# Where operand tiles land, the order of a block's seven products, an in-place tanh, and the order of matmuls and mixer steps in a hybrid decoder layer

## The chip, the core and the metric

The kernel runs on one core of one Trainium2 chip. The metric is the device time of one execution in microseconds (us). Three executions of the kernel before took 2190.18 (median), 2188.14 and 2193.57 us. One further execution was recorded by the hardware profiler; it took 2188.96 us, of which the profile's span covers 2186.9 us.

## What is computed

One decoder layer over 2048 tokens of width 1024, in float32, followed by a final norm:

```python
h = modulate(rmsnorm(x, norm1_w), shift1, scale1)
proj = h @ w_in                                  # q, k, v, z, xbc, dt
attn = sliding_window_attention(rope(q), rope(k), v, sinks)    # window 128
xbc  = silu(causal_depthwise_conv(xbc, conv_w, conv_b))
y    = ssd_chunked_scan(xs, dt, A, Bm, Cm, d_skip)             # chunks of 128
y    = group_rmsnorm(y * silu(z)) * ssm_norm_w
x    = x + gate1 * (concat([attn, y]) @ w_out)
h = modulate(rmsnorm(x, norm2_w), shift2, scale2)
g, u = split(h @ w_gate_up)                      # 1024 -> 2 x 2816
x    = x + gate2 * ((silu(g) * u) @ w_down)
out  = rmsnorm(x, final_norm_w)
```

Shifts, scales and gates come from a small projection of `c`. The change touches the projection `z` (the "gates" below), and the first of the two feed-forward products, `h @ w_gate_up`.

## The kernel before

**Tiles and numbers.** The tokens are worked on in four blocks of 512 (`T`). A float32 product is made of three matmuls on pairs of reduced-precision tiles: an operand is split into a high part (the copy, ScalarE) and a low part (the rest, mostly VectorE), and `mm3` or `product` adds high*high, high*low and low*high in one PSUM bank. So every operand costs one ScalarE instruction and one VectorE or GpSimd instruction per 128x512 tile: `halves` for weights (L897 the high part, L898 the low part), `kept` (L931, L932) and `shifted` (L926, L927) for the feed-forward operands.

**Projections and the mixer beside them.** For each block, the projections (queries, keys and values, convolution, gates) run as generators that stop (`yield`) after each piece. Between two pieces, `tick(ratio)` advances the mixer's generators by `ratio` steps on average: attention and the state-space scan of an earlier block. Of attention, a step transposes the keys (L623, into the PSUM bank `am`) and the queries (L628, bank `at`), ScalarE and VectorE split both (L624 and L625 to the tile `k_ring`, L631 and L632 to a tile `m`), and the scores follow (L663, banks `am` and `at`). VectorE masks the scores (L672), ScalarE takes exponentials and scales them (L685, L691), the probabilities are transposed (L697 on TensorE, copied out of PSUM by ScalarE at L699) and multiplied by the values (L706, copied out at L708). L791 and L806 are the scan's matmuls, L735 and L736 its running sums, L208 a product of the adaLN projection that VectorE makes beside all this, L850/L851 and L278/L279 splits of other operands.

**The gates.** `gated(b, h)` makes z for a block in `two_parts`: two passes over half of the depth, each of two parts of two pieces. A piece has 24 matmuls, and the first pass has four pieces. Each finished 128x256 tile goes through ScalarE (tanh, L538) and VectorE (L539) and is stored to memory (L540). The tanh went to a tile of the ring "s", which has three buffers of 128x512 and serves the convolution, the rotary embedding and the feed-forward's sums too; L539's result went to a staged tile "so" of a ring of six.

**The feed-forward's quads.** `quad(s, f, ...)` makes one 512-wide column block f (22 of them) for a pair s of token blocks (s=0: blocks 0 and 1, s=1: blocks 2 and 3) in a seven-product scheme of the Strassen kind. It loads four weight tiles (L903), forms sums of them (L1059, L1060, L1064, L1066, tiles of the ring "s" ), splits them into seven pairs w11, w12, ws1..ws4, w22 (L897, L898), and multiplies each with one of seven operands (b11, b21, t1, t2, t3, b22, t4): 7 x 12 matmuls of 128x512 on L1049, L1050 and L1051. ScalarE copies out the first product (L1073), a tanh of the second (L1077), and the third product (L1081). With `fresh`, which was set for f=0 of both pairs, the last four products are written k by k rather than product by product. For s=0 the operands b11, b21 and t1 are ready early, and the other four (t2, t3, b22, t4) are computed ahead and wait in memory: for k=0..2 as `raw_d`, for k=3 in tiles of the ring "t" (eight buffers, `tmp()`). `operands_kept` loads them after quad 0 has been begun: three tiles of t2 into three tiles of the ring "t" (L1015), then their conversions, then three tiles of t3, and so on. Weight loads of quad 1 are issued after the last of these loads.

**What sets the order.** On TensorE the order up to the end of block 3's gates is the order of the code (`tc.manual_schedule`, L1544). From the quads on, and on the other engines nearly everywhere, a scheduler with a timeline model orders the instructions of each engine; a tile that comes out of a ring has to wait until the last reader of the buffer's earlier content is done. Around the gates of block 2 the code was: `take(g, 4)`, that is, all four pieces of the first pass, and then four times `tick(MIX2)`. MIX2 is 1.1: so many mixer steps each tick makes on average. PSUM has four banks "d" for the dense products and one each of `am`, `at`, `sm`, `st` for the mixer.

Of the kernel before, what the change touches and what calls it, by code (L numbers as in the profile page):

```python
# [45 lines left out]
def hymba_layer(ctx, tc, xT, xtok, pos, wada, wadk, vecs, rows, wq, wkv, wz, wx, wo, wgu, wd, outT):  # L46
# [11 lines left out]
    def big(tag, bufs, dt=F32, pool=sb):  # L58
        return pool.tile([P, T], dt, name=tag, tag=tag, bufs=bufs)
# [14 lines left out]
    def tmp():  # L74
        return big("t", TMP, pool=fw)
# [315 lines left out]
    def staged():  # L391
        return small([P, 256], "so", 6, pool=ip)
# [141 lines left out]

    def gated(b, h):
        def gate(part, t, ps):
            z, th = staged(), big("s", 3, pool=fw)[:, 0:256]
            nc.scalar.activation(th, ps, AF.Tanh, scale=0.5)  # L538
            nc.vector.scalar_tensor_tensor(z, th, 1.0, ps, ALU.add, ALU.mult)  # L539
            nc.sync.dma_start(z_d[b * NT + t][:, part * 256:part * 256 + 256], z)  # L540
        yield from two_parts(b, h, "z", wz, gate)

# [351 lines left out]
    def halves(x, eng):  # L894
        two = wt.tile([P, 2, 528], F32R, name="w", tag="w", bufs=SPLIT)
        hi, lo = two[:, 0, 0:T], two[:, 1, 0:T]
        nc.scalar.activation(hi, x, AF.Copy)  # L897
        eng.tensor_tensor(lo, x, hi.bitcast(F32), ALU.subtract)  # L898
        return hi, lo
# [29 lines left out]
    def kept(into, x, eng=nc.gpsimd):  # L929
        hi, lo = into  # L930
        nc.scalar.activation(hi, x, AF.Copy)  # L931
        eng.tensor_tensor(lo, x, hi.bitcast(F32), ALU.subtract)  # L932
# [75 lines left out]
                yield  # L1008

    def operands_kept(ops):  # L1010
        for n, src in zip(("t2", "t3", "b22", "t4"), (2, 1, 0, 3)):
            got = []
            for k in range(3):
                x = tmp()
                scaled.last = nc.sync.dma_start(x, raw_d[k][src])  # L1015
                got.append(x)
            for k, x in enumerate((*got, sums_ahead.last[n])):
                if n == "b22":
                    shifted(ops[n][k], x, shift_of(k, 1))
                else:  # L1020
                    kept(ops[n][k], x, nc.gpsimd if n == "t4" else nc.vector)

    def operands_last(s, ops, bc):

# [19 lines left out]
    def product(out, a, b, first, ks=range(4)):  # L1044
        for k in ks:
            ks = slice(k * P, (k + 1) * P)
            ahi, alo = a[0][:, ks], a[1][:, ks]
            bhi, blo = b[k]
            nc.tensor.matmul(out, ahi, bhi, start=first and k == 0, stop=False, skip_group_check=True)  # L1049
            nc.tensor.matmul(out, ahi, blo, start=False, stop=False, skip_group_check=True)  # L1050
            mm3.last = nc.tensor.matmul(out, alo, bhi, start=False, stop=k == 3, skip_group_check=True)  # L1051

    def quad(s, f, ops, banks, fresh, behind):
        with tc.issue_after(scaled.last.ins) if behind else nullcontext():
            a11, a21, a22, a12 = (load_w(wgu[f, u, half]) for u, half in ((0, 0), (1, 0), (1, 1), (0, 1)))
        w11 = halves(a11, nc.vector)
        w12 = halves(a12, nc.vector)
        s1, s2, s3, s4 = (big("s", 3, pool=fw) for _ in range(4))
        nc.vector.tensor_tensor(s1, a21, a22, ALU.add)  # L1059
        nc.vector.tensor_tensor(s2, s1, a11, ALU.subtract)  # L1060
        ws1 = halves(s1, nc.vector)
        ws2 = halves(s2, nc.vector)
        other = nc.gpsimd if s else nc.vector
        other.tensor_tensor(s3, a11, a21, ALU.subtract)  # L1064
        ws3 = halves(s3, nc.vector)
        other.tensor_tensor(s4, a12, s2, ALU.subtract)  # L1066
        ws4 = halves(s4, nc.vector)
        w22 = halves(a22, nc.vector)

        pa, pb, pc, pd = banks  # L1070
        u2, u3, c22 = tmp(), tmp(), tmp()
        product(pa, w11, ops["b11"], True)
        nc.scalar.activation(u2, pa, AF.Copy)  # L1073
        yield
        product(pa, w12, ops["b21"], False)
        g1, g2 = tmp(), tmp()
        nc.scalar.activation(g1, pa, AF.Tanh, scale=0.5)  # L1077
        nc.vector.scalar_tensor_tensor(g1, g1, 1.0, pa, ALU.add, ALU.mult)
        yield
        product(pc, ws1, ops["t1"], True)  # L1080
        nc.scalar.activation(c22, pc, AF.Copy)  # L1081
        yield
        turns = ((pb, ws2, "t2", True), (pd, ws3, "t3", True), (pc, ws4, "b22", False), (pa, w22, "t4", True))
        if fresh:
            for k in range(4):
                for out, w, name, new in turns:
                    product(out, w, ops[name], new, (k,))
                if k < 3:
                    yield

        def turn(i):
            if not fresh:
                out, w, name, new = turns[i]
                product(out, w, ops[name], new)

        def keep(name, x):
            nc.sync.dma_start(act_d[s][name][f // 2], x)
        turn(0)
        nc.vector.tensor_tensor(u2, u2, pb, ALU.add)
        yield  # L1100
        turn(1)
        nc.vector.tensor_tensor(u3, u2, pd, ALU.add)
        nc.gpsimd.tensor_tensor(c22, c22, u3, ALU.add)
        yield
        turn(2)
        nc.vector.tensor_tensor(u2, u2, pc, ALU.add)
        nc.scalar.activation(g2, u2, AF.Tanh, scale=0.5)
        nc.vector.scalar_tensor_tensor(g2, g2, 1.0, u2, ALU.add, ALU.mult)
        nc.gpsimd.tensor_tensor(g2, g2, c22, ALU.mult)
        if f % 2:  # L1110
            b11, b12 = held[s]
            keep("b22", g2)
            nc.vector.tensor_tensor(b12, g2, b12, ALU.subtract)
            keep("t3", b12)
            nc.vector.tensor_tensor(b11, b11, b12, ALU.add)
            keep("t2", b11)
        yield
        turn(3)
        nc.vector.tensor_tensor(u3, u3, pa, ALU.add)
        nc.vector.tensor_tensor(g1, g1, u3, ALU.mult)  # L1120
        if f % 2:
            keep("b21", g1)
            nc.vector.tensor_tensor(u3, g1, b11, ALU.subtract)
            keep("t4", u3)
        else:
            keep("b11", g1)
            nc.vector.tensor_tensor(u3, g2, g1, ALU.subtract)
            keep("t1", u3)
            held[s] = g1, g2
        yield  # L1130
# [413 lines left out]
    with tc.manual_schedule(engines={mybir.EngineType.PE}):  # L1544
# [31 lines left out]
        finish(mix0)  # L1576
        mix = []
        g = gated(2, h)
        take(g, 4)
        for _ in range(4):  # L1580
            tick(MIX2)
        split = mixed(0, mix, range(KT), lambda c: operand())
        for _ in beside(g, MIX1):
# [53 lines left out]
    def quads(s, ops, banks, behind, before_last=None):  # L1637
        for f in range(NF):
            if before_last and f == NF - 1:
                before_last()  # L1640
            yield from quad(s, f, ops, banks(f), f == 0, f == behind)

    bp = early.enter_context(tc.tile_pool(name="b0l", bufs=1, reuse_waits="tile"))
    operand_tiles(ops, bp, ("b22", "t3", "t2", "t4"))
# [172 lines left out]
```

## Time and profile before

| | |
|---|---|
| three runs | 2190.18 (median), 2188.14, 2193.57 us |
| profiled execution | 2188.96 us, span 2186.9 us |
| granted TensorE clock, mean | 0.993 |
| TensorE busy (matmul) | 2140.5 us, 98% of the span |
| VectorE busy | 1669.6 us, 76% |
| ScalarE busy | 1017.8 us, 47% |
| GpSimd busy | 547.5 us, 25% |
| DMA | 466.76 MB, mean 213 GB/s |

TensorE is PE in the views, VectorE DVE, ScalarE ACT, GpSimd POOL; SPq is the queue from which SyncE issues transfers. A row of the timeline is: start, duration, engine, line, operation, the tiles written and read, the shape, how many; and in brackets the idle time of the engine before it with the instruction that ended it. Matmuls are pipelined: a row's duration is the time of one through the array, and the distance between two starts is what one costs.

### The profile page before, as it was taken

The numbers are of one execution on the slowest core, as the hardware profiler recorded it, in microseconds if no ns is written. First come the engines' busy times: TensorE is split into PE (matmuls) and PEld (weight loads), VectorE is DVE, ScalarE is ACT, GpSimd is POOL, SyncE is SP. The second block draws the span as 40 slices with busy tenths as digits, with TensorE's granted clock in tenths as the row PEclk, the third lists the DMA queues.
The fourth block names the chain that finished last, engine by engine and source line by source line (L and its number), as shares of the span: only waits on it lengthen the run. The fifth ranks groups of instructions, "written<-read, shape, count | busy, mean of one in ns | idle before, by whom it ended". The sixth has DMA issues, their size and how long they took to land.

```text
span 2186.9 us, 33266 instructions
## 1 busy us (share of the span) xinstructions
PE 2140.5 (98%) x10984; PEld 1763.5 (81%) x10984; DVE 1669.6 (76%) x3195; ACT 1017.8 (47%) x2137; POOL 547.5 (25%) x658
## 2 busy tenths in 40 slices
PE   8989999899999999999999999999999999999998
PEld 6888897788777777778888888788888888788887
DVE  7978857875777876789888679778888775786575
ACT  3776635653556545334344445433333334554441
POOL 0213443222111211243331222333333230210011
PEclk8999999999999999999999999999999999999999
DMA  7798988797998322333324778645555536678553
GB/s 280 240 341 309 345 267 296 243 334 239 356 361 294 116 99 89 125 102 122 125 92 159 243 259 286 226 138 190 171 171 181 167 115 233 231 259 281 184 163 103
DMA packets 287708, 466.76 MB, mean 213 GB/s; under 512 B 27440, under 2 KB 97072, under 8 KB 287536
## 3 DMA queue, kind: packets, MB, share of 16 engines
q1 hardware_dynamic: 286960, 464.13, 63.5%
q8 instruction: 86, 1.41, 0.3%
q14 instruction: 86, 0.70, 0.1%
q10 hardware_dynamic: 576, 0.52, 0.1%
HBM read 329.73 MB, written 134.81 MB: 212 GB/s over the span
## 4 chain that ended last, share of the span: by engine, by line
PE 79%; DVE 9%; DMA 6%; ACT 3%; issue 3%; POOL 1%; SPq 0%; DVEq 0%; ACTq 0%; POOLq 0%
PE d L1181 15%; PE d L1049 9%; PE d L1050 9%; PE d L1051 9%; PE d L286 5%; PE d L287 5%; PE d L288 5%; PE d L1322 1%; PE am L1051 1%; PE am L1049 1%; PE am L1050 1%; PE am L706 1%; DMA a<-act_t 1%; PE sm L1051 1%; PE sm L1050 1%
## 5 line engine op out<-in xcount | busy, mean ns | idle before, releaser
L1181 PE MATMUL d<-a,w 128*128 128x512 f32 x1716 | 402.3, 395 | 3.6 <-DVE w L1177 2.1
L1181 PEld LDWEIGHTS d<-a,w 128*128 128x128 f32 x1716 | 321.8, 188 | 81.3 <-DVE w L1177 2.9
L1049 PE MATMUL d<-b,w 128*128 128x512 f32 x924 | 366.1, 399 | 5.0 <-ACT t L1081 3.0
L1050 PE MATMUL d<-b,w 128*128 128x512 f32 x924 | 367.4, 398 | 0.2 <-DVE b L932 0.2
L1051 PE MATMUL d<-b,w 128*128 128x512 f32 x924 | 366.2, 398 | 0.2 <-DVE w L898 0.2
L1049 PEld LDWEIGHTS d<-b,w 128*128 128x128 f32 x924 | 174.1, 188 | 45.2 <-ACT t L1081 3.5
L1050 PEld LDWEIGHTS d<-b,w 128*128 128x128 f32 x924 | 174.3, 189 | 40.8 <-DVE b L932 0.8
L1051 PEld LDWEIGHTS d<-b,w 128*128 128x128 f32 x924 | 173.9, 188 | 39.4 <-DVE w L898 0.5
L897 ACT ACTIVATE w<-s 128x512 fp32r<-128x512 f32 x176 | 110.9, 632 | 203.2 <-PE d L1051 146.0
L286 PE MATMUL d<-w,hl 128*128 128x256 f32 (+1 forms) x592 | 172.1, 291 | 2.7 <-DVE s L511 2.7
L287 PE MATMUL d<-w,hl 128*128 128x256 f32 (+1 forms) x592 | 167.2, 282 | 0.0
L288 PE MATMUL d<-w,hl 128*128 128x256 f32 (+1 forms) x592 | 167.0, 282 | 0.0
L898 DVE TENSOR_TENSOR w<-s,w 128x512 fp32r<-128x512 f32 x176 | 156.9, 893 | 7.1 <-ACT w L897 5.9
L1163 DVE TENSOR_TENSOR a<-a 128x512 fp32r<-128x512 f32 x154 | 112.0, 739 | 49.2 <-ACT a L1162 48.8
L897 ACT ACTIVATE w<-raw 128x512 fp32r<-128x512 f32 x132 | 83.1, 631 | 132.5 <-PE d L1051 54.1
L1177 DVE TENSOR_TENSOR w<-raw,w 128x512 fp32r<-128x512 f32 x156 | 109.8, 713 | 39.0 <-ACT w L1176 37.0
L1162 ACT ACTIVATE a<-a 128x512 fp32r<-128x512 f32 x154 | 95.6, 628 | 88.8 <-DMA a<-act_t 50.9
L296 POOL TENSOR_TENSOR acc<-acc,t 128x512 f32<-128x512 f32 x35 | 52.5, 1499 | 319.6 <-ACT t L295 308.9
L286 PE MATMUL d<-hl,w 128*128 128x512 f32 x320 | 131.6, 411 | 0.3 <-DVE stp L565 0.3
L1176 ACT ACTIVATE w<-raw 128x512 fp32r<-128x512 f32 x156 | 90.6, 587 | 84.3 <-PE d L1181 51.5
L288 PE MATMUL d<-hl,w 128*128 128x512 f32 x320 | 126.1, 394 | 0.0
L287 PE MATMUL d<-hl,w 128*128 128x512 f32 x320 | 125.8, 393 | 0.0
(421 smaller groups left out, 4782.0 us busy)
## 6 DMA issues: line engine op xcount, KB each, us to landing
raw<-in_wgu_dram SPq DMA_DIRECT2D x176, 256.0 KB, 2.9
act_t<-t SPq DMA_DIRECT2D x88, 256.0 KB, 3.1
a<-act_t SPq DMA_DIRECT2D x88, 256.0 KB, 4.3
act_b<-t SPq DMA_DIRECT2D x66, 256.0 KB, 2.0
a<-act_b SPq DMA_DIRECT2D x66, 256.0 KB, 4.2
aw<-in_wada_dram SPq DMA_DIRECT2D x64, 256.0 KB, 5.1
w<-w_x SPq DMA_DIRECT2D x32, 512.0 KB, 5.7
raw<-wd_s SPq DMA_DIRECT2D x64, 256.0 KB, 3.0
```

The costliest lines, as they stand in the source:

```text
L286: nc.tensor.matmul(out, ahi, bhi, start=first, stop=False)
L287: nc.tensor.matmul(out, ahi, blo, start=False, stop=False)
L288: mm3.last = nc.tensor.matmul(out, alo, bhi, start=False, stop=last)
L897: nc.scalar.activation(hi, x, AF.Copy)
L898: eng.tensor_tensor(lo, x, hi.bitcast(F32), ALU.subtract)
L1049: nc.tensor.matmul(out, ahi, bhi, start=first and k == 0, stop=False, skip_group_check=True)
L1050: nc.tensor.matmul(out, ahi, blo, start=False, stop=False, skip_group_check=True)
L1051: mm3.last = nc.tensor.matmul(out, alo, bhi, start=False, stop=k == 3, skip_group_check=True)
L1162: nc.scalar.activation(hi, raw, AF.Copy)
L1163: nc.vector.tensor_tensor(lo, raw, hi.bitcast(F32), ALU.subtract)
L1177: nc.vector.tensor_tensor(w[1], raw, w[0].bitcast(F32), ALU.subtract)
L1181: mm3.last = nc.tensor.matmul(ps, w[x][:, ws], act[k][y], start=new and k == 0 and x + y == 0, stop=k == KP - 1 and x == 1, skip_group_che ...
```

## The change

Four edits. Line numbers after the first edited function's loop shift by one or more: L1049 to L1051 become L1050 to L1052, L1081 (the copy of ws1 times t1) becomes L1077, and L1077 (the tanh of the product with w12) becomes L1081.

1. `operands_kept` loads the twelve raw tiles straight into the place of the low part of their own pair (the tiles "b"), all twelve loads first (now L1014), and the conversions after them. The ring "t" is no longer used for them; the tiles for k=3 stay as they were.
2. In `quad`, the product ws1 times t1 comes second and w12 times b21 third, and w12 is split after ws1. `fresh` is set for f=0 of s=1 alone.
3. The gates' tanh is written to the staged tile "so", and VectorE's instruction works in place. The ring "s" is not used there any more.
4. Around the gates of block 2, each of the first pass's four pieces is followed by one tick, instead of four pieces and then four ticks.

```diff
     def gated(b, h):
         def gate(part, t, ps):
-            z, th = staged(), big("s", 3, pool=fw)[:, 0:256]
-            nc.scalar.activation(th, ps, AF.Tanh, scale=0.5)
-            nc.vector.scalar_tensor_tensor(z, th, 1.0, ps, ALU.add, ALU.mult)
+            z = staged()
+            nc.scalar.activation(z, ps, AF.Tanh, scale=0.5)
+            nc.vector.scalar_tensor_tensor(z, z, 1.0, ps, ALU.add, ALU.mult)
...
     def operands_kept(ops):
-        for n, src in zip(("t2", "t3", "b22", "t4"), (2, 1, 0, 3)):
-            got = []
+        names = tuple(zip(("t2", "t3", "b22", "t4"), (2, 1, 0, 3)))
+        for n, src in names:
             for k in range(3):
-                x = tmp()
-                scaled.last = nc.sync.dma_start(x, raw_d[k][src])
-                got.append(x)
-            for k, x in enumerate((*got, sums_ahead.last[n])):
+                scaled.last = nc.sync.dma_start(ops[n][k][1].bitcast(F32), raw_d[k][src])
+        for n, _ in names:
+            eng = nc.gpsimd if n == "t4" else nc.vector
+            for k in range(4):
+                x = ops[n][k][1].bitcast(F32) if k < 3 else sums_ahead.last[n]
                 if n == "b22":
                     shifted(ops[n][k], x, shift_of(k, 1))
                 else:
-                    kept(ops[n][k], x, nc.gpsimd if n == "t4" else nc.vector)
+                    kept(ops[n][k], x, eng)
...
         w11 = halves(a11, nc.vector)
-        w12 = halves(a12, nc.vector)
         s1, s2, s3, s4 = (big("s", 3, pool=fw) for _ in range(4))
         nc.vector.tensor_tensor(s1, a21, a22, ALU.add)
         nc.vector.tensor_tensor(s2, s1, a11, ALU.subtract)
         ws1 = halves(s1, nc.vector)
+        w12 = halves(a12, nc.vector)
...
+        product(pc, ws1, ops["t1"], True)
+        nc.scalar.activation(c22, pc, AF.Copy)
+        yield
         product(pa, w12, ops["b21"], False)
         g1, g2 = tmp(), tmp()
         nc.scalar.activation(g1, pa, AF.Tanh, scale=0.5)
         nc.vector.scalar_tensor_tensor(g1, g1, 1.0, pa, ALU.add, ALU.mult)
-        yield
-        product(pc, ws1, ops["t1"], True)
-        nc.scalar.activation(c22, pc, AF.Copy)
         yield
...
         g = gated(2, h)
-        take(g, 4)
         for _ in range(4):
+            take(g, 1)
             tick(MIX2)
...
-            yield from quad(s, f, ops, banks(f), f == 0, f == behind)
+            yield from quad(s, f, ops, banks(f), s == 1 and f == 0, f == behind)
```

Two places show how the instructions move. The first is VectorE's queue beside the gates of block 2, where L625 makes the low part of the transposed keys. Before, it stands there like this (from the end of the convolution, L501, on):

```order
L501 SCALAR_TENSOR_TENSOR sx<-sx,s 128x512
L279 TENSOR_TENSOR w<-raw,w 128x512
L851 TENSOR_TENSOR hl_5248<-hl_5248 128x512
L851 TENSOR_TENSOR hl_5250<-hl_5250 128x512
L279 TENSOR_TENSOR w<-raw,w 128x512
L793 TENSOR_TENSOR m_5170<-st,ex 128x512
L727 TENSOR_TENSOR m_5597<-upper,ahi 128x512
L208 ISA aw,part<-aw,csil,vec 128x512
L208 ISA part 128x1
L625 TENSOR_TENSOR k_ring<-am,k_ring 128x128
L632 SCALAR_TENSOR_TENSOR m_5189<-at,m_5189 128x512
```

In the changed kernel the same stretch of VectorE's queue reads:

```order
L793 TENSOR_TENSOR m_5074<-st,ex 128x512
L727 TENSOR_TENSOR m_5573<-upper,ahi 128x512
L687 TENSOR_TENSOR ast<-ast 128x4
L688 RECIPROCAL ast<-ast 128x4
L501 SCALAR_TENSOR_TENSOR sx<-sx,s 128x512
L625 TENSOR_TENSOR k_ring<-am,k_ring 128x128
L632 SCALAR_TENSOR_TENSOR m_5119<-at,m_5119 128x512
L279 TENSOR_TENSOR w<-raw,w 128x512
L740 TENSOR_TENSOR m_5158<-m_5158,m_4907 128x512
L851 TENSOR_TENSOR hl_5232<-hl_5232 128x512
L208 ISA aw,part<-aw,csil,vec 128x512
```

L625 and L632 have moved ahead of L279, L851 and L208, and stand directly behind L501. On TensorE, the four ticks' instructions (L791, then L623 and L628, then L735 and L736, then L663) stood together behind the 96 matmuls; now each group follows 24 of them, so that 48 of the 96 lie between the transposes L623/L628 and the scores L663.

The second place is ScalarE's queue in quad 0, from the last of the raw tiles of t3 to the copy of ws1 times t1 (L1081 before, the tile "d" is the PSUM bank). Before, with L1077 the tanh of the product with w12:

```order
L931 ACTIVATE b<-t 128x512 x4
L708 COPY m_8892<-am 128x256
L699 COPY m_9071<-at 128x4x128
L926 ACTIVATE b<-t,mod 128x512 x2
L699 COPY m_9071<-am 128x4x128
L926 ACTIVATE b<-t,mod 128x512 x2
L699 COPY m_9129<-at 128x4x128
L1077 ACTIVATE t<-d 128x512
L931 ACTIVATE b<-t 128x512
L1081 ACTIVATE t<-d 128x512
```

In the changed kernel, from the copy of the first product (L1074) on; the copy of ws1 times t1 is L1077 and the tanh of the product with w12 is L1081:

```order
L1074 ACTIVATE t<-d 128x512
L1077 ACTIVATE t<-d 128x512
L685 ACTIVATE m_8973,ast<-m_8973,ast 128x256 x2
L685 ACTIVATE m_8976,ast<-m_8976,ast 128x256 x2
L686 ACTIVATE ast<-ast 128x4
L699 COPY m_9006<-am 128x4x128
L691 ACTIVATE m_8973<-m_8973,ast 128x256 x2
L691 ACTIVATE m_8976<-m_8976,ast 128x256 x2
L699 COPY m_9006<-at 128x4x128
L931 ACTIVATE b<-b 128x512 x2
L1081 ACTIVATE t<-d 128x512
```

The copy of ws1 times t1 stood behind thirteen of the sixteen conversions of operands (L931 and L926, of which the rows above show the last nine); now it stands right behind the copy of the first product, ahead of the first conversion. In SyncE's queue the twelve operand loads (L1014) now follow each other with nothing between them, and the loads of quad 1's weights (L903) follow. In the quads from the second on, TensorE's order had the product with w12 behind that with ws1 (or ws2) already, and quad 0's last four products were already in the order product by product.

## Prediction

> **What bounds the kernel now.** I read the page's first part, then TensorE's waits over the whole span, then the stretches around the two long ones that lie where the change is, and there the timeline.
>
> ```profile
> PE 2140.5 (98%) x10984; PEld 1763.5 (81%) x10984; DVE 1669.6 (76%) x3195; ACT 1017.8 (47%) x2137; POOL 547.5 (25%) x658
> ```
>
> TensorE is the bound: of 2186.9 us it is without a matmul for 46.4 only. The change removes no matmul, so it can gain at most where TensorE waits or runs at a lower clock. TensorE's longest wait (total, times, longest):
>
> ```profile
> PE am L663 <- DVE k_ring L625: 4.8, 2, 4.7
> ```
>
> This row heads the list; its 4.7 lie in the gates of block 2 (edit 4). Two follow that belong to the opening, which the change leaves alone; the fourth, 3.0, lies in quad 0 (edits 1 to 3; its row is below). The stretches (busy time of PE, PEld, DVE, ACT, POOL; granted clock; DMA share):
>
> ```profile
> 122.00:128.00 6.00, 3.07 (x25) 2.69 (x23) 6.00 (x11) 4.93 (x14) 3.19 (x3) 1.00 1.02 352
> 384.70:396.29 11.59, 11.59 (x98) 11.59 (x97) 6.96 (x25) 10.39 (x31) 1.61 (x3) 1.00 0.74 239
> 396.29:405.00 8.71, 3.90 (x25) 2.94 (x23) 8.58 (x13) 4.04 (x9) 2.85 (x2) 0.92 0.98 328
> 680.56:696.30 15.74, 14.37 (x80) 10.90 (x78) 15.17 (x36) 11.64 (x36) 0.00 (x0) 1.00 0.89 306
> 696.30:717.00 20.70, 16.62 (x76) 11.58 (x77) 15.02 (x19) 16.90 (x34) 8.70 (x7) 0.92 0.63 210
> 1560.00:1620.00 60.00, 60.00 (x260) 48.64 (x260) 50.28 (x71) 20.21 (x34) 18.34 (x12) 1.00 0.59 185
> ```
>
> The first row is for the clock, below. The 96 gate matmuls run without a gap up to 396.29; then, for 8.71 us, TensorE is busy for 3.90. In quad 0's first 36.4 us it is idle for 1.37 + 4.08 = 5.45. In a steady quad (the last row) it never stops.
>
> **Edit 4, the gates.** TensorE's timeline behind the 96 matmuls:
>
> ```profile
> 397.15 0.27 PE L623 MATMUL am<-ident,m 128*128 128x128 f32 x1
> ...
> 397.93 0.40 PE L736 MATMUL sm<-m,later_r 128*128 128x512 f32 x1
> 402.99 0.35 PE L663 MATMUL am<-k_ring,m 64*128 64x256 f32 x1 [4.66 <-DVE k_ring L625]
> ...
> 405.02 0.58 PE L286 MATMUL d<-w,hl 128*128 128x256 f32 x1
> ...
> 407.06 0.28 PE L286 MATMUL d<-w,hl 128*128 128x256 f32 x1
> ```
>
> The same twelve scores one step earlier, where nothing held them:
>
> ```profile
> 383.79 0.39 PE L663 MATMUL am<-k_ring,m 64*128 64x256 f32 x1
> ...
> 384.69 0.39 PE L286 MATMUL d<-w,hl 128*128 128x256 f32 x1
> ```
>
> Three costs: the wait, 4.66. The scores, 405.02 - 402.99 = 2.03 instead of 384.69 - 383.79 = 0.90, that is 1.13. The next nine matmuls, 407.06 - 405.02 = 2.04 instead of 9 x 0.12 (the 96 before take 11.59) = 1.08, that is 0.96. Together 6.75 us. Why L625 was late shows VectorE's timeline:
>
> ```profile
> 394.20 0.69 DVE L501 SCALAR_TENSOR_TENSOR sx<-sx,s 128x512 f32<-128x512 f32 x1
> ...
> 400.88 1.75 DVE L208 CUSTOM_DVE_ANT_0 aw<-aw,csil,vec 128x512 f32<-128x512 f32 x1
> ...
> 402.56 0.28 DVE L625 TENSOR_TENSOR k_ring<-am,k_ring 128x128 fp32r<-128x128 f32 x1
> ...
> 404.56 0.74 DVE L208 CUSTOM_DVE_ANT_0 aw<-aw,csil,part 128x512 f32<-128x512 f32 x1
> ...
> 405.84 0.47 DVE L672 CUSTOM_DVE_ANT_0 m<-am,amask,row 128x256 f32<-128x256 f32 x1
> ```
>
> The keys were transposed at 397.15 only, and then L625 stood behind seven instructions of other work (L279 to L208, in the order above). In the changed order the transposes come after 48 of the 96 matmuls, about 5.7 us earlier than the last of them, and L625 and L632 stand directly behind L501, which ends at 394.9: they are done by about 396. The scores' place on TensorE is after the same matmuls as before, at about 397.93 + 0.40 = 398.3. So 2 us of cover is left, and the whole 6.75 go. The cover is made of the last 48 matmuls; without it the transposes would again have to pass through ScalarE and VectorE while TensorE stands.
>
> What is late next: the transposes of probabilities L697 write to the banks that L672 has to have read. TensorE comes to them at 398.3 + 0.9 + 24 x 0.12 + 0.9 for L806 = 403.0. In VectorE's new order L672 stands behind both L208, whose transfer is needed first. If L208 again begins at 400.88 and takes 1.75, the second of 0.74, one more split of about 0.6 and two L672 of 0.47 follow, and L697 could start at 404.9, a wait of 1.9; if the weights of L208 have landed earlier, it is nothing. I take 1.1, above the middle, since L208 still stands ahead of L672. Edit 4: 6.75 - 1.1 = **5.7 us** gained, between 3 (the wait of 1.9, and a second one of its size in the same step) and 6.8.
>
> **The clock.** In this trace a wait of 3.05 us and one of 4.66 are followed by matmuls at about half the rate, for some 3.8 us, and one of 2.75 is not. The rows of the first and of the third, whose granted clock stays 1.00 (first row of the stretches):
>
> ```profile
> 710.52 0.61 PE L1049 MATMUL d<-b,w 128*128 128x512 f32 x1 [3.05 <-ACT t L1081]
> ...
> 714.28 0.39 PE L1049 MATMUL d<-b,w 128*128 128x512 f32 x1
> ```
> ```profile
> 125.34 0.39 PE L286 MATMUL d<-w,hl 128*128 128x256 f32 x1 [2.75 <-DVE s L511]
> ```
>
> At 710.52 nine matmuls take 714.28 - 710.52 = 3.76, where 60.00 / 260 = 0.231 each (steady quad) would make 2.08: 1.68 lost. By the rows the limit lies between 2.75 and 3.05 us of idling, so the waits of up to 2 us that I leave in the changed kernel cost only themselves. [...]
>
> **Edits 1 to 3, quad 0.** TensorE's waits from 680 to 717:
>
> ```profile
> PE d L1049 <- ACT t L1081: 3.0, 1, 3.0
> PE d L1049 <- ACT b L931: 1.2, 2, 0.7
> PE d L1049 <- ACT w L897: 0.3, 1, 0.3
> PE am L706 <- ACT m L699: 0.3, 1, 0.3
> PE d L1051 <- DVE w L898: 0.2, 1, 0.2
> PE d L1050 <- DVE b L932: 0.2, 1, 0.2
> ```
>
> 5.2 us, and 1.68 for the clock: 6.9. The longest is for the copy of ws1 times t1. SyncE's and ScalarE's timelines:
>
> ```profile
> 690.06 9.43 SPq L1015 DMA_DIRECT2D t<-raw_t x6
> ...
> 705.81 2.02 SPq L903 DMA_DIRECT2D raw<-in_wgu_dram  x4
> ```
> ```profile
> 697.70 1.70 ACT L691 ACTIVATE m<-m,ast 128x256 f32<-128x256 f32 x4
> ...
> 707.16 1.33 ACT L926 ACTIVATE b<-t,mod 128x512 fp32r<-128x512 f32 x2 [0.82 <-DMA t<-raw_b]
> ...
> 709.88 0.59 ACT L1081 ACTIVATE t<-d 128x512 f32<-128x512 f32 x1
> ```
>
> Six loads take 9.43 us to be issued, because each from the fourth on waits until a buffer of the ring "t" has been converted; ScalarE stands before the conversions, and the copy stands behind them. Edit 1 gives each tile its own place, so twelve loads can be issued one behind the other (at the issue time of a single one, below 0.5 us, that is at most 6 us from 690 or a little earlier; it took 9.43 for six), and the last lands some 4 us later, at about 698. Edit 2 puts the copy ahead of all conversions. Edit 3 frees the ring "s" of the tanh, so that quad 0's sums and splits no longer wait for the last gate tiles; this takes the 0.3 and 0.2 at L897 and L898. I count the first three rows and the last two, 4.9, and the clock, 1.7, as gone: 6.6.
>
> What is late next is ScalarE's attention work, since the conversions and copies were moved around it: TensorE reaches L706 and L697 some 5 us earlier than before, while the exponentials before them (L685, L691) begin when the scores come. By the changed order L697 stands right behind the scores of the same step; two L672 of 0.47 lie between, so about 1.0 is lost. The wait at L706, 0.3 now, may grow by the 1.7 that four L691 take on ScalarE, or go; I take 0.7 more. Edits 1 to 3: 6.6 - 1.0 - 0.7 = **4.9 us**, between 1 (the wait comes back at the same place, but short enough for the clock to stay) and 7. GpSimd's four L932 for t4 and the loads of quad 1's weights behind the twelve loads cost nothing: these weights were issued from 705.81 on, with quad 1 beginning behind 717, and now stand behind loads that are issued by about 696. One load of keys (L611), which waits for a copy on GpSimd, stands among them now; it would have to hold them for more than 8 us to be felt.
>
> **The steady quads.** Edit 2 moves w12's split behind ws1's in each of 44 quads. TensorE's order there had that already, and VectorE is busy for 50.28 of 60 us with TensorE not waiting: nothing, plus or minus 1. The tanh in place costs nothing by itself: as many instructions of the same shape. The k-by-k order was undone by the scheduler in quad 0 anyway.
>
> **The sum.** 5.7 + 4.9 = 10.6 against the profiled execution's own 2188.96: 2178.4. The runs' median is 1.2 above that execution, so 2179.6 is the forecast.
>
> **The rivals.** First, *one stall only goes*: the other is replaced by its next limit (L672 behind L208 at the gates, or ScalarE's queue in quad 0). For it: both queues are full there (ScalarE 16.90 of 20.70, VectorE 8.58 of 8.71). Against it: the replaced wait would have to be as long, while the rows between are 0.4 to 1.7 each. It gives 2190.2 - 5.7 = 2184.5 or 2190.2 - 4.9 = 2185.3.
>
> Second, *neither goes*, or the edits do not do what they say: the scheduler's model may expect loads at times that the chip doesn't keep, so that a transfer under the 0.89 DMA share at 680 to 696 lands late, and ScalarE's first conversion holds what stands behind it. 2190, same.
>
> Third, *slower*: the splits in the 22 quads of s=1. VectorE has 9.7 us of 60 to spare, about 20 us per quad, so 3.3 us in each; when w12's pair, now later, comes after its matmuls want it, each quad waits. At 0.5 us in each of 21 quads the gain of 10.6 is used up; at 1 us the time is 2179.6 + 21 = 2200.6. Against it: 260 matmuls in 60.00 us without a gap, with that product third already.
>
> Fourth, *more*: the waits for L672 vanish too, at the gates and in quad 0: 2190.2 - 6.8 - 6.9 = 2176.5, and a little less where later steps gain by starting earlier.
>
> **How the numbers follow.** Forecast 0.57, one stall 0.25, neither 0.08, slower 0.05, more 0.05. A difference of 0.3%, 6.6 us, is about what a measurement of this kernel can tell from no change; faster means below 2183.6. The forecast's own range, 2176 to 2184 (the smaller gain at one of the two places), lies nearly all below; of one stall, a third. So faster 0.57 x 0.95 + 0.25 x 0.33 + 0.05 = 0.67; slower 0.05; same 0.28. The range from 2174 to 2187 holds forecast, one stall and most of more; it leaves out neither and slower.
>
> **What would show it.** Right: no wait of over 2 us on TensorE between 380 and 410, L663 at about 398.3, TensorE's granted clock 1.00 there; no wait for the copy of ws1 times t1 (now L1077); L1014 issued within some 5 us; L685 in the place of L1081 on the critical chain. Wrong: a wait of over 3 us for L1014's transfers or for L931, a granted clock under 1.00 after 690, or a wait per quad from 1200 us to 1660.

## The result and the profile after

The changed kernel takes 2178.67 us (median of six runs, 2177.24 to 2179.82) against 2191.78 us for the kernel before, measured beside it: the ratio of the two is 0.9945, with a 95% interval from 0.9934 to 0.9955, so by the ratio 12.1 us or 0.55% faster. The profiled execution took 2179.79 us (span 2177.7), the upper end of its runs.

TensorE's waits over the whole span no longer hold either of the two rows on which the prediction was built (total, times, longest):

```profile
PE at L337 <- DVE t L331: 3.3, 1, 3.3
PE st L778 <- DVE m L767: 3.0, 3, 1.5
```

These are the second and third; the first, 4.7, and the second belong to the opening, as before. The third, 3.0 in three waits, was 1.2 in two before.

The gates of block 2, on TensorE and on VectorE. The step begins with scores at 386.60 here and at 383.79 before, so 2.81 us have to be taken off for a comparison:

```profile
394.24 0.27 PE L623 MATMUL am<-ident,m 128*128 128x128 f32 x1
...
397.86 0.39 PE L736 MATMUL sm<-m,later_r 128*128 128x512 f32 x1
...
401.09 0.38 PE L663 MATMUL am<-k_ring,m 64*128 64x256 f32 x1
...
404.99 1.02 PE L806 MATMUL st<-m,m 128*128 128x256 f32 x4
405.85 0.60 PE L697 MATMUL am<-ident,m 128*128 128x128 f32 x4
```
```profile
397.74 0.69 DVE L501 SCALAR_TENSOR_TENSOR sx<-sx,s 128x512 f32<-128x512 f32 x1
398.35 0.29 DVE L625 TENSOR_TENSOR k_ring<-am,k_ring 128x128 fp32r<-128x128 f32 x1
...
403.11 0.75 DVE L208 CUSTOM_DVE_ANT_0 aw<-aw,csil,part 128x512 f32<-128x512 f32 x1
...
404.39 0.48 DVE L672 CUSTOM_DVE_ANT_0 m<-am,amask,row 128x256 f32<-128x256 f32 x1
```

The scores L663 begin without a wait at 401.09 - 2.81 = 398.28; the prediction said 398.3. L625 was done 2.4 us ahead of them, L632, the other operand, 1.9. From the earlier scores to L806 it is 404.99 - 386.60 = 18.39 us, where it was 408.82 - 383.79 = 25.03 before: 6.6 us less. L672 began at 404.39 behind both L208, yet L697 did not wait: TensorE came to it at 405.85 only.

Part of this is given back at once. TensorE's waits from 410 to 445, and the instruction of VectorE that holds the longest of them:

```profile
PE st L751 <- DVE m L793: 1.5, 1, 1.5
PE am L697 <- DVE ast L672: 0.8, 1, 0.8
PE am L623 <- ACT m L708: 0.5, 1, 0.5
...
```
```profile
433.79 0.75 DVE L208 CUSTOM_DVE_ANT_0 aw<-aw,csil,vec 128x512 f32<-128x512 f32 x1 [1.11 <-DMA aw<-in_wada_dram]
...
434.54 0.68 DVE L793 TENSOR_TENSOR m<-st,ex 128x512 f32<-128x512 f32 x1
```

Before, this stretch had 1.0 us of waits, both at L697, and these are still there; now it has 3.2, with two of 0.2 that are left out here. New are the 1.5 at L751 and 0.7 for ScalarE's copy L708. TensorE is ahead by some 6 us, while L208 still waits for its transfer and L793 stands behind it.

Quad 0. SyncE's loads, ScalarE's copy of ws1 times t1 (L1077 now) and its first conversion, and TensorE's waits from 676 to 715:

```profile
687.77 4.30 SPq L1014 DMA_DIRECT2D b<-raw_t  x6
692.17 1.33 SPq L1014 DMA_DIRECT2D b<-raw_b  x3
693.74 1.65 SPq L1014 DMA_DIRECT2D b<-raw_t  x3
```
```profile
688.74 0.60 ACT L1077 ACTIVATE t<-d 128x512 f32<-128x512 f32 x1
...
694.82 1.15 ACT L931 ACTIVATE b<-b 128x512 fp32r<-128x512 f32 x2
```
```profile
PE am L697 <- DVE ast L672: 1.1, 1, 1.1
PE d L1052 <- DVE w L898: 0.6, 1, 0.6
PE d L1051 <- DVE b L932: 0.5, 1, 0.5
```

All twelve loads are out in 7.6 us, where six took 9.4. Counted from quad 0's first matmul, the copy begins 19 us earlier (10.4 us behind it instead of 29.3). Of 5.2 us of waits 2.2 are left, and the largest is the one that was forecast to come, L697 behind its own step's scores, with 1.1 for 1.0. From the first matmul of quad 0 to the 85th of the quads it is 33.55 us, 38.07 before: 4.5 us less. Not all of this is saved: 70 matmuls of the mixer lie between these two marks, 78 lay there before. At the 186th matmul of the quads 111 matmuls of the mixer, the same ones, lie behind in both kernels, and there the changed kernel is 3.7 us ahead.

One thing lies far from the change. Before, TensorE waited three times near 1872 us, in the last stage of the second pair of blocks; in the changed kernel it doesn't wait there at all. TensorE's waits from 1855 to 1885, and VectorE, before:

```profile
PE d L1181 <- DVE w L1177: 2.1, 2, 1.6
PE d L1181 <- ACT w L1176: 0.3, 1, 0.3
```
```profile
1870.93 0.69 DVE L1246 TENSOR_TENSOR u<-u,d 128x512 f32<-128x512 f32 x1 [3.89 <-PE d L1181]
1871.65 0.75 DVE L1212 SCALAR_TENSOR_TENSOR x<-u,mod,x 128x512 f32<-128x512 f32 x1
1872.32 0.55 DVE L1177 TENSOR_TENSOR w<-raw,w 128x384 fp32r<-128x384 f32 x1
```

and VectorE after (L1178 is that split, L1247 that eviction):

```profile
1861.76 0.55 DVE L1178 TENSOR_TENSOR w<-raw,w 128x384 fp32r<-128x384 f32 x1
1865.35 0.69 DVE L1247 TENSOR_TENSOR u<-u,d 128x512 f32<-128x512 f32 x1 [3.04 <-PE d L1182]
```

Before, the split of a weight tile stands behind an eviction (VectorE's instruction that reads a PSUM bank) that waits 3.9 us for TensorE, and TensorE then waits for the split. After, the split stands ahead of the eviction. At the three waits the starts of neighbouring matmuls lie 2.8 us further apart before than at full rate; with the steps of 0.34 instead of 0.23 us beside them it is 3.3 from 1855 to 1885. After, it is 0.1.

### The profile page after: what moved, and what is told of

It reads as the page before. It is cut to its first block, busy times and chain, and to the rows that moved or that the text cites. A ratio compares the mean times of both kernels' runs of the same rounds, so it can differ in the third digit from the quotient of the medians.

```text
span 2177.7 us, 33314 instructions
## 1 busy us (share of the span) xinstructions
PE 2139.7 (98%) x10984; PEld 1764.9 (81%) x10984; DVE 1651.1 (76%) x3195; ACT 1016.5 (47%) x2137; POOL 553.5 (25%) x658
## 4 chain that ended last, share of the span: by engine, by line
PE 79%; DVE 8%; DMA 5%; ACT 3%; issue 2%; POOL 1%; SPq 0%; DVEq 0%; ACTq 0%; POOLq 0%
PE d L1182 17%; PE d L1052 9%; PE d L1051 9%; PE d L1050 9%; PE d L286 4%; PE d L287 4%; PE d L288 4%; DMA aw<-in_wada_dram 1%; PE d L1323 1%; PE am L1050 1%; PE am L1052 1%; PE am L1051 1%; PE am L706 1%; PE sm L1052 1%; PE sm L1051 1%
## 5 line engine op out<-in xcount | busy, mean ns | idle before, releaser
L1052 PE MATMUL d<-b,w 128*128 128x512 f32 x924 | 366.9, 399 | 0.6 <-DVE w L898 0.6
L1051 PE MATMUL d<-b,w 128*128 128x512 f32 x924 | 366.6, 397 | 0.7 <-DVE b L932 0.5
L1050 PE MATMUL d<-b,w 128*128 128x512 f32 x924 | 363.2, 397 | 0.0
L897 ACT ACTIVATE w<-s 128x512 fp32r<-128x512 f32 x176 | 111.0, 631 | 237.2 <-PE d L1052 148.2
L1051 PEld LDWEIGHTS d<-b,w 128*128 128x128 f32 x924 | 174.2, 189 | 41.7 <-DVE b L932 1.5
L1052 PEld LDWEIGHTS d<-b,w 128*128 128x128 f32 x924 | 173.8, 188 | 40.4 <-DVE w L898 1.0
L1050 PEld LDWEIGHTS d<-b,w 128*128 128x128 f32 x924 | 174.2, 189 | 38.0
L286 PE MATMUL d<-w,hl 128*128 128x256 f32 (+1 forms) x592 | 171.9, 290 | 2.7 <-DVE s L511 2.7
L288 PE MATMUL d<-w,hl 128*128 128x256 f32 (+1 forms) x592 | 166.8, 282 | 0.0
L1178 DVE TENSOR_TENSOR w<-raw,w 128x512 fp32r<-128x512 f32 x156 | 114.0, 739 | 43.3 <-ACT w L1177 43.0
L1104 POOL TENSOR_TENSOR t<-t 128x512 f32<-128x512 f32 x44 | 75.5, 1717 | 277.0 <-DVE t L1103 126.1
L1164 DVE TENSOR_TENSOR a<-a 128x512 fp32r<-128x512 f32 x154 | 106.2, 704 | 46.1 <-ACT a L1163 45.3
L898 DVE TENSOR_TENSOR w<-s,w 128x512 fp32r<-128x512 f32 x176 | 131.1, 746 | 6.3 <-ACT w L897 5.4
L286 PE MATMUL d<-hl,w 128*128 128x512 f32 x320 | 131.6, 411 | 0.0
L288 PE MATMUL d<-hl,w 128*128 128x512 f32 x320 | 126.1, 394 | 0.0
L1177 ACT ACTIVATE w<-raw 128x512 fp32r<-128x512 f32 x156 | 90.6, 587 | 75.8 <-PE d L1182 44.3
```

The source lines that it names most:

```text
L286: nc.tensor.matmul(out, ahi, bhi, start=first, stop=False)
L1164: nc.vector.tensor_tensor(lo, raw, hi.bitcast(F32), ALU.subtract)
L1178: nc.vector.tensor_tensor(w[1], raw, w[0].bitcast(F32), ALU.subtract)
```

## The experiments

All kernels were timed against the kernel before on the same chip. "Gates" is the time from a matmul of block 2's convolution (376.07 in the kernel before) to the first of quad 0, "quad 0" that from there to the 85th matmul of the quads, each from the profiled execution and as the difference to before (304.49 and 38.07 us). "Same work" is the same difference at a matmul of the quads where the same matmuls of the mixer lie behind in both kernels (near the 186th; only1 and no3 have no such point with the kernel before and are reckoned by way of the changed kernel). The last column is whether TensorE waits for a weight's split near 1870 us.

| kernel | edits | median us | ratio to before, 95% | gates | quad 0 | same work | wait near 1870 |
|---|---|---|---|---|---|---|---|
| changed | 1 2 3 4 | 2178.67 | 0.9945 (0.9934 to 0.9955) | -4.7 | -4.5 | -3.7 | no |
| only4 | 4 | 2184.22 | 0.9976 (0.9966 to 0.9986) | -5.1 | +3.0 | +1.7 | yes |
| only123 | 1 2 3 | 2181.19 | 0.9961 (0.9948 to 0.9973) | -0.3 | -5.2 | -5.3 | no |
| only1 | 1 | 2188.61 | 0.9992 (0.9983 to 1.0000) | 0.0 | -2.4 | -0.4 | yes |
| only3 | 3 | 2186.74 | 0.9988 (0.9980 to 0.9997) | -0.5 | +2.1 | +0.8 | yes |
| only2 | 2 | 2187.05 | 0.9992 (0.9982 to 1.0001) | -0.2 | +3.3 | +2.1 | no |
| no1 | 2 3 4 | 2182.98 | 0.9972 (0.9961 to 0.9982) | -6.5 | +1.4 | +0.4 | no |
| no2 | 1 3 4 | 2185.01 | 0.9977 (0.9969 to 0.9986) | -6.1 | -0.5 | -0.3 | yes |
| no3 | 1 2 4 | 2179.25 | 0.9954 (0.9941 to 0.9967) | -5.0 | -3.8 | -1.8 | no |
| cover1 | all, less cover | 2177.36 | 0.9934 (0.9920 to 0.9947) | -5.5 | -4.5 | -3.7 | no |
| s1old | 1 3 4, and 2 at s=0 only | 2181.24 | 0.9955 (0.9942 to 0.9968) | -5.7 | -4.5 | -3.7 | yes |
| s0old | 1 3 4, and 2 at s=1 only | 2182.03 | 0.9958 (0.9946 to 0.9971) | -5.1 | -1.0 | -0.7 | no |
| freshboth | all, k by k twice | 2176.14 | 0.9930 (0.9917 to 0.9944) | -4.7 | -4.5 | -3.7 | no |

**Edit 4 alone, and all but it.** The kernel before with

```diff
-        take(g, 4)
         for _ in range(4):
+            take(g, 1)
             tick(MIX2)
```

> Edit 4 alone (gates' pieces and ticks alternated). Theory, two stalls that add: the 4.66 us wait at L663 and the half-rate matmuls behind it go (6.75 us at the place), of which the steps up to 430 us give back 1 to 3 us as in the changed kernel; quad 0 keeps its 3 us wait. So 4 to 6 us faster than before, ratio 0.9973 to 0.9982. Rival, one place carries all: 11 to 12 us faster, or none because the time is given back by quad 0.

and the changed kernel without these lines:

> Edits 1 to 3 without edit 4. Theory: the wait at 402.99 stays as it was (4.6 us, granted clock under 1), quad 0's 6.9 us shrink to about 2; 4.5 to 5.5 us faster than before, ratio 0.9975 to 0.998. Rival (one place carries): no difference, or all 12 us.

Edit 4 alone gives 0.24%, 5.3 us, as expected; TensorE has no wait left between 396 and 412. (In quad 0 it is not the 3.0 us wait that stays: others, 5.6 us together, stand in its place.) Edits 1 to 3 give 0.39%, 8.5 us, more than expected, with the wait at the gates still at the head of TensorE's waits:

```profile
PE am L663 <- DVE k_ring L625: 4.8, 2, 4.6
```

5.3 + 8.5 = 13.8 is as much as the 12.1 of all four within the intervals. The two places add, as far as these intervals can tell. Beyond quad 0's 5.3 us, edits 1 to 3 have the 3.3 us near 1870.

**Each of edits 1 to 3 alone.** The code of the edits is that of the change.

> Edit 1 alone: the raw operand tiles into their own place, all twelve loads first. Theory: the loads were what ScalarE's queue stood for, so the copy of ws1 times t1 is no longer late although it still stands behind conversions: the 3.05 us wait falls below 1 us and the slow matmuls go; 3 to 5 us faster. Rival, the order on ScalarE's queue is what matters (edit 2): the wait at the copy stays over 2 us, under 2 us faster.

> Edit 3 alone: the gates' tanh in place. Theory: quad 0's sums come earlier by the three buffers, which takes the 0.3 and 0.2 us waits at L897 and L898 and nothing else: 0 to 1 us faster. Rival: the ring held the whole of quad 0 back, and 3 us or more go.

> Edit 2 alone: ws1 times t1 second, w12's split after ws1, no k-by-k order for the first pair. Theory after the first four runs (edits 1 and 3 alone each gave under 4 us, edits 1 to 3 together 8 to 9): each of the three takes one of several waits in quad 0 that stand behind each other, and the copy's place on ScalarE's queue is the largest; 3 to 5 us faster alone, with the waits at L931 larger in place of the one at the copy. Rival: without edit 1 the operands come as late as before, and under 1 us goes.

Each alone gave 1.8 to 2.6 us with intervals that reach to 0 or nearly so; the theory's 3 to 5 us for edit 1, and again for edit 2, were wrong. Edit 3 alone gave 2.6 us where 0 to 1 was expected, and its quad 0 is no shorter; where that comes from is open. With edit 1 alone the wait for the copy goes, as its theory has it, but others stand in its place (L932 1.7, L931 1.1, L706 0.9): 4.4 us in all, 5.2 before. For edit 2 the reason shows in TensorE's waits of only2 from 680 to 721, and in ScalarE's queue there (L1076 is the copy of ws1 times t1 in this kernel):

```profile
PE d L1049 <- ACT t L1076: 3.1, 1, 3.1
PE d L1049 <- ACT b L931: 1.4, 2, 1.1
PE d L1050 <- DVE b L932: 0.9, 2, 0.7
...
```
```profile
710.24 1.34 ACT L926 ACTIVATE b<-t,mod 128x512 fp32r<-128x512 f32 x2 [1.46 <-DMA t<-raw_b]
711.48 0.61 ACT L931 ACTIVATE b<-t 128x512 fp32r<-128x512 f32 x1
712.00 0.57 ACT L1076 ACTIVATE t<-d 128x512 f32<-128x512 f32 x1
```

The product comes second in the code, but the scheduler still puts its copy behind the conversions that wait for the trickling loads. So edit 2 without edit 1 does not move the copy. (Why the scheduler does so was not tried.)

**Each of them left out.**

> The changed kernel without edit 1 (operands through the ring of temporaries, three at a time). Theory: the loads' trickle returns, and waits for L931 or L926 of 2 to 4 us stand in quad 0; 2 to 4 us slower than the changed kernel, 8 to 10 us faster than before (ratio 0.9955 to 0.9965). Rival, edit 2 is enough: within 1 us of the changed kernel (0.9945).

> The changed kernel without edit 2. Theory: the copy of ws1 times t1 again stands behind the conversions on ScalarE's queue, a wait of 1 to 3 us for it returns; 2 to 4 us slower than the changed kernel, 8 to 10 us faster than before (0.9955 to 0.9965). Rival: with the operands early the copy's place does not matter, within 1 us of the changed kernel.

> The changed kernel without edit 3 (the tanh in the ring that the quads' sums use). Theory: 0.5 to 2 us slower than the changed kernel, with waits for L897 and L898 at quad 0's start; 10 to 12 us faster than before (0.9945 to 0.9955). Rival: the ring holds quad 0 back by 3 us or more once the other waits are gone (0.996 or above).

Without edit 1 or without edit 2 the time is that of edit 4 alone, within 1 us: 0.9972 and 0.9977 beside 0.9976. That is 6 and 7 us above the changed kernel, more than the 2 to 4 expected (no2 lacks the 3.3 us near 1870 too). Without edit 3 it is 0.9954, inside the changed kernel's interval. In no1 it is not for L931 that TensorE mainly waits, as expected, but at L706, L897 and L697 (2.3, 1.8 and 1.1). no2 shows the other half of the pair: the loads are early, as in the changed kernel, and TensorE now waits for the first conversion, because ScalarE has not got to it:

```profile
688.21 0.60 PE L697 MATMUL at<-ident,m 128*128 128x128 f32 x4
692.48 0.80 PE L1050 MATMUL d<-b,w 128*128 128x512 f32 x1 [3.67 <-ACT b L931]
```
```profile
689.24 1.71 ACT L691 ACTIVATE m<-m,ast 128x256 f32<-128x256 f32 x4 [0.50 <-DVE ast L688]
690.85 0.58 ACT L1078 ACTIVATE t<-d 128x512 f32<-128x512 f32 x1
691.33 0.58 ACT L1082 ACTIVATE t<-d 128x512 f32<-128x512 f32 x1
691.81 0.62 ACT L931 ACTIVATE b<-b 128x512 fp32r<-128x512 f32 x1
```

The scaling of probabilities, a tanh and a copy out of PSUM stand ahead of the conversion. In the kernels with edits 1 and 2 at s=0 (six of them) quad 0 is 1.8 to 5.3 us shorter at the same work; in the seven others it lies between 0.7 us shorter and 2.1 longer, each with another wait. Neither the loads nor the order of the products pays alone. The 1.8 is no3's, without edit 3; with it the five others have 3.7 or more. So edit 3 seems to add to the pair, but only in single profiles: in time, no3 is 2.0 us above the changed kernel, which the intervals cannot tell from nothing.

**Less cover at the gates.** The changed kernel with

```diff
-        for _ in range(4):
-            take(g, 1)
+        for n in (3, 0, 1, 0):
+            take(g, n)
             tick(MIX2)
```

> The changed kernel, but around the gates of block 2 three pieces, two ticks, the fourth piece, two ticks: 24 matmuls (2.9 us) instead of 48 (5.7 us) lie between the transposes and the scores, where before there were none. Theory, what counts is the cover: the wait of 4.66 us at L663 shrinks to between 0.5 and 2 us, the granted clock there stays 1.00, and the time is 0 to 2 us above the changed kernel's (ratio 0.9945 to 0.9955). Rival, the order of VectorE's queue alone decides: L851 and L279 stand ahead of L625 again, the wait is 3 us or more with half-rate matmuls behind it, and 4 to 5 us of the gain are lost (0.9965).

In VectorE's queue four instructions (L793, L727, L279 and L851) stand between L501 and L625 again. TensorE's waits from 396 to 412:

```profile
PE am L663 <- DVE k_ring L625: 0.7, 1, 0.7
PE at L663 <- DVE m L632: 0.2, 1, 0.2
```

0.9 us instead of 4.9, at full clock (the L286 to L288 behind the scores start 0.12 us apart). The rival, that VectorE's order alone decides, falls: with four instructions ahead of L625 one piece of 24 matmuls hides nearly all. But cover is not the only thing that differs from the kernel before: three of the seven instructions that stood ahead of L625 there, L208 among them, now stand behind it, and L625 begins 3.3 us earlier, counted from the convolution. A kernel with the old order on VectorE and the new cover was not tried. The time, 0.9934, isn't above the changed kernel's.

**Where edit 2 works far away.** The changed kernel with edit 2's two moves (the split of w12, the second product) made conditional on s:

```diff
+        early12 = s == 1
+        if early12:
+            w12 = halves(a12, nc.vector)
         s1, s2, s3, s4 = (big("s", 3, pool=fw) for _ in range(4))
...
+        if not early12:
+            product(pc, ws1, ops["t1"], True)
+            nc.scalar.activation(c22, pc, AF.Copy)
+            yield
         product(pa, w12, ops["b21"], False)
```

This is s1old, with the old order at s=1; in s0old the first line has `s == 0`, and the k-by-k writing is set for both pairs as before.

> The changed kernel with the old order of products and splits in the quads of the second pair of blocks (s=1) alone. Theory from the eight runs so far: VectorE's queue at the second pair's last stage has the split of a 384-wide weight tile behind an eviction that waits for TensorE in every kernel without edit 2, and ahead of it in every kernel with it; it is s=1's order that shifts it. So the three waits for that split near 1870 us (2.8 us together) come back, quad 0 stays as in the changed kernel: 2 to 3.5 us slower than the changed kernel (0.9955 to 0.9962). Rival: it was edit 2 at s=0, and nothing changes (0.9945).

> The changed kernel with the old order in the quads of the first pair (s=0) alone, quad 0 among them. Theory: the waits near 1870 us stay away; in quad 0 the copy of ws1 times t1 or an operand's conversion is waited for by 1 to 3 us; 2 to 5 us slower than the changed kernel (0.9955 to 0.9967). Rival, quad 0's gain comes from edits 1 and 3 and edit 2 helped only far away: within 1 us of the changed kernel.

Both came out as the theory has it. With the old order at s=1 alone the wait returns, and the median is 2.6 us above the changed kernel's. TensorE's waits of s1old from 1855 to 1885 (its lines are 9 higher):

```profile
PE d L1191 <- DVE w L1187: 2.0, 2, 1.6
PE d L1191 <- ACT w L1186: 0.3, 1, 0.3
```

With the old order at s=0 alone these waits stay away, quad 0 keeps 0.7 of its 3.7 us (TensorE waits 3.7 for a conversion, L931, more than the 1 to 3 expected), and the median is 3.4 us above. The intervals of both overlap with the changed kernel's. But all five runs of each lie above all five of cover1 and of freshboth, which were timed beside them on the same chip, with medians 4 to 6 us lower. So edit 2 gains twice: in quad 0 together with edit 1, and near 1870, some 40 us behind the last of the quads of s=1, by an order of two instructions on VectorE that no line of the change names. That the scheduler moved them is shown; why it did is not.

**The k-by-k writing.** The changed kernel with

```diff
-            yield from quad(s, f, ops, banks(f), s == 1 and f == 0, f == behind)
+            yield from quad(s, f, ops, banks(f), f == 0, f == behind)
```

> The changed kernel with the k-by-k writing of the last four products set for f=0 of both pairs again. Theory: the scheduler's order of quad 0's matmuls is the same either way, only the mixer's steps begin three stops earlier: within 2 us of the changed kernel (0.994 to 0.9955). Rival: the k-by-k writing was what made quad 0 wait for all four operands at once, and over 2 us of the gain go. For all four runs, of the clock: in the nine profiles so far a stretch of 3.413 us, on one fixed grid per run, in which TensorE was busy for less than 0.40 was followed by half clock each time (16 of 16), and from 0.47 to 0.8 in 6 of 93 only. The same should hold here.

Quad 0 is as long as in the changed kernel (33.58 and 33.55 us), so this part of edit 2 does nothing there. The kernel's 0.9930 is the best ratio measured and lies below the range expected, but its interval overlaps the changed kernel's; both are clearly faster than the kernel before.

## Why the prediction was right, and where it was not

- **The gates.** Right in mechanism and size: the wait, the slow scores and the slow matmuls went, 6.6 us for the 6.75 forecast. The 1.1 us that I left for L697 behind L672 did not come there; 2.2 us more waits than before came 15 to 35 us later (1.5 for L793 behind L208, 0.7 for L708). Net, by quad 0's start, 4.7 for the 5.7 forecast; the other kernels with edit 4 have 4.7 to 6.5, so this is as near as single profiles can tell. How much of it is the cover and how much the new order on VectorE was not separated.
- **Quad 0.** 3.7 at the same work for the 4.9 forecast, and right in what is late next (L697, 1.1 for 1.0). The make-up was not right throughout: the half clock whose 1.7 was counted as gone came back at another place of quad 0; the extra 0.7 at L706 does not show as a wait, for a reason given in the next point; and splits and conversions (L898, L932) took 1.1. The twelve loads took 7.6 us to issue, not some 5: a single one took 0.32 to 0.76 us where the median before was 0.32, and landed after 5.2 us in the median, 3.6 before. The working gave edit 1, edit 2 and edit 3 each a share. The runs show no such shares: 1 and 2 are worth 1.8 us together, 3.7 with edit 3, and next to nothing apart.
- **The clock.** The step "the limit lies between 2.75 and 3.05 us of idling, so the waits of up to 2 us that I leave in the changed kernel cost only themselves" failed. In the changed kernel half clock follows a wait of 1.1 us in quad 0 and one of 2.2 us near 1367:

```profile
686.03:689.45 3.42, 2.45 (x18) 2.07 (x17) 2.09 (x8) 1.73 (x4) 1.04 (x1) 1.00 1.05 377
689.45:692.86 3.41, 3.30 (x10) 2.84 (x11) 1.94 (x8) 2.76 (x11) 0.00 (x0) 0.50 1.01 362
1365.29:1368.70 3.41, 1.28 (x6) 1.06 (x7) 3.41 (x6) 2.53 (x5) 0.26 (x1) 1.00 1.05 387
1368.70:1372.12 3.42, 3.42 (x10) 2.65 (x9) 3.42 (x7) 1.67 (x3) 2.29 (x1) 0.50 0.62 222
```

  (columns as in the prediction: busy time of PE, PEld, DVE, ACT, POOL; granted clock; DMA share.) A granted clock under 1.00 after 690 was one of the prediction's own signs of being wrong. That the half clock cost nothing in quad 0 all the same is luck. cover1 has the same code there, runs it at full clock, and needs 33.57 us for 33.55. TensorE's waits of cover1 from 674 to 715:

```profile
PE am L706 <- ACT m L699: 1.5, 1, 1.5
PE am L697 <- DVE ast L672: 1.1, 1, 1.1
...
```

  The first of these the changed kernel does not have: its slow matmuls fill the time in which TensorE would wait for ScalarE's copy. That ScalarE's attention work is late next, as the prediction says of L706, is so; the slow matmuls hid it. Whether the 1.7 us at 710.52 in the kernel before were lost in full is not shown.
- **The steady quads.** "Nothing, plus or minus 1" was right for the quads (84 matmuls in 19.4 to 19.5 us in both kernels) and wrong for what follows them: 3.3 us came from the reorder near 1870, which the sum has no term for.
- **The sum.** 10.6 forecast, 12.1 measured (9.9 to 14.5 by the interval): gates 4.7 and quad 0 3.7 in place of 5.7 and 4.9, and 3.3 that was not in the sum, together 11.7. The two places that were reasoned about gave 8.4 of the 10.6; that the total came out on the forecast's side is in part luck, the 3.3. The two profiled executions themselves lie 9.2 us apart only, mainly because the opening of the changed one took 2.2 us longer (last section).
- **The rivals.** One stall only, neither, and slower did not happen; there is no wait per quad between 1200 and 1660 us. Of *more*, half happened: the wait for L672 at the gates did not come, the one in quad 0 did.

## What to carry to other kernels

A chain of transposes, splits and matmuls needs other matmuls between its links, and one piece of them, 2.9 us here, did nearly as well as two. An early load and an early place on the queue of the engine that converts it pay only together: with either one missing, 4.4 to 6.1 us of waits stood in quad 0, mostly at other places than the 5.2 before. When two kernels are compared from one matmul to another, count what else was done between: here 0.8 of 4.5 us was work that had only moved. In a kernel whose queues a scheduler orders, compare the waits of the whole span after an edit; here a quarter of the gain arose 1150 us behind quad 0, in two instructions that the change does not name.

## What the runs showed of the hardware that was not expected

**The clock's grid.** In each of the fourteen profiles the granted clock changes only at points 3.413 us apart, on a grid that keeps its phase over the whole execution; the phase differs from run to run. In the kernel before it changes at 403.57, 406.98, 710.77 and 714.18 (from the second to the third 303.79, 89 such lengths), in the changed kernel at 689.45, 692.86, 1368.70 and 1372.12 (675.84, 198). How busy TensorE was within one such stretch tells more in these profiles than the length of the wait. The kernel no2 shows it: a wait of 3.46 us at 140.8 that falls into two stretches, each half busy, is not followed by half clock, while one of 3.67 that fills a stretch is followed by half clock for two of them:

```profile
139.09:142.50 3.41, 1.71 (x15) 1.47 (x13) 3.12 (x18) 3.41 (x15) 0.00 (x0) 1.00 1.05 402
142.50:145.91 3.41, 1.66 (x15) 1.69 (x16) 2.67 (x8) 2.42 (x8) 0.00 (x0) 1.00 1.06 396
145.91:149.33 3.42, 3.42 (x34) 3.15 (x33) 2.33 (x6) 1.02 (x2) 0.00 (x0) 1.00 1.06 364
688.63:692.05 3.42, 0.18 (x2) 0.00 (x0) 1.58 (x4) 2.92 (x9) 0.00 (x0) 1.00 0.95 323
692.05:695.46 3.41, 2.98 (x9) 1.51 (x11) 2.30 (x5) 3.41 (x8) 0.00 (x0) 0.50 1.04 398
695.46:698.88 3.42, 3.42 (x14) 2.29 (x11) 3.42 (x6) 3.42 (x8) 1.94 (x2) 0.50 0.81 290
```

Over the first ten profiles, between the opening and 2150 us, half clock followed each of the 16 stretches that were busy for less than 0.40, and 6 of the 108 between 0.40 and 0.80 (the expectation above said 93, a miscount). In the last four, which were not used to find this, it followed 3 of 3 and 4 of 38. In the kernel before it is 2 of 2 and 0 of 12, in the changed kernel 1 of 1 (0.38, at 1365.29) and 1 of 10. The wait of 2.75 us at 125.34 in the kernel before, busy 0.51 in its stretch, fits, and so do the two that were slow there, 0.13 and 0.11. The changed kernel's own stretch in quad 0, 0.72, is one of these exceptions, so busy time alone does not explain it; s1old has one of 0.83 at the same place. Of the 18 matmuls in the changed kernel's stretch 12 are the scores L663, `64*128` in their rows where the dense products have `128*128`. Whether that is why was not tried.

**The opening.** Five of the fourteen profiles have a stretch of full clock at 7 to 12 us, and the first projection matmul starts at 33.98 to 34.44; in the nine others it starts at 35.79 to 36.67, whatever the kernel. The kernel before is one of the five (from 7.60 to 10.60 13 matmuls in 1.79 us of busy time, start at 34.44), the changed kernel one of the nine (6 in 1.79, start at 36.67). The opening is the same code in all of them, so about 2 us of the difference between two single profiles can be this.
